# One-hot operands of the gate-matrix products: the token in front of the key, written per token

## The chip, the cores and the metric

The kernel runs on 1 core of one Trainium2 chip. The metric is device time in microseconds (us) of one execution, as the median of several runs. Engines are named as in the profile: PE is TensorE (PEld its weight loads), DVE VectorE, ACT ScalarE, POOL GpSimd, SP the engine that issues most DMAs; a q behind the name is the engine's instruction queue.

## What is computed

A float32 network on 512 tokens of 1024 channels: first two layers of short convolution and retention (with 16 meta tokens in front), then a block with two gated linear-attention mixers, and last a retrieval layer (PEER) with 16384 experts of one neuron each, and a final norm. Only the retrieval layer touches the change. Cut to that:

```python
def peer_ffn(xn, w_q, sub_keys, u, v):
    q = (xb @ w_q).reshape(128, 8, 2, 128)                    # block of 128 tokens, 8 heads, 2 sides
    s = jnp.einsum('thpd,hpnd->thpn', q, sub_keys)            # 128 sub-keys a side
    s_top, i_top = lax.top_k(s, 16)
    cand = s_top[:, :, 0, :, None] + s_top[:, :, 1, None, :]
    cand_idx = i_top[:, :, 0, :, None] * 128 + i_top[:, :, 1, None, :]
    best, pos = lax.top_k(cand.reshape(128, 8, 256), 16)
    expert = jnp.take_along_axis(cand_idx.reshape(128, 8, 256), pos, axis=-1)
    g = jax.nn.softmax(best, axis=-1)
    act = jax.nn.gelu(jnp.einsum('td,thkd->thk', xb, u[expert]), approximate=False)
    return jnp.einsum('thk,thkd->td', g * act, v[expert])
```

So each token has 128 chosen experts (8 heads by 16), each named by a first and a second key (0 to 127 each) and carrying a weight g.

## The kernel before

The 512 tokens are four tiles of 128. For the first three (NDENSE = 3) all 128 x 128 experts are computed as dense products and then weighed by a gate matrix that is zero where an expert wasn't chosen; for the last tile the chosen experts are gathered from DRAM. An "expert" e in the code is a group of 128 experts with the same first key.

Weights stream from DRAM in pieces of 128 x 1024 (class `Weights`); each piece is one task. A list of generators, the background, is advanced between tasks and between chunks of a product (`tick`), so many steps a piece as `PACE` says for the phase, always the generator at the head of the list. That gives the order of the work in the program; a scheduler that simulates the engines puts each engine's instructions in their final order, in which each engine then runs them.

The stage in question lies between the second block and the experts' phase. Three things share it:

- `top_k(i, b, sc)` ranks the keys of tile i, on DVE with small steps on ACT. `weights(i)` ends it: it transposes first keys, second keys and weights of tile i on PE (L1412) so that the 128 chosen experts lie on the partitions and the 128 tokens along the row, and writes them as float16 into `picks[i]` (keys k1 and k2, the weight in two parts w). Then it puts `gate_matrix(i)` into the background.
- `gate_matrix(i)` builds each token's matrix of 128 second keys by 128 first keys. With the chosen experts on the partitions, a one-hot matrix of the second keys, transposed, times a one-hot matrix of the first keys that is weighed by g gives that matrix by one product for each part of the weight. `rows(t0)` (L1437) compares a table `it16` of 0 to 127 with the keys of eight tokens, `weighed(t0, oh)` (L1444) multiplies the first keys' rows by both weight parts, `product(t0, oh)` (L1451) multiplies for four tokens, two products each into one bank of PSUM, and `store(t0, ps)` (L1460) copies the bank into a staging tile on ACT and writes 16 tokens at a time to DRAM (`gate_d`, L1464, on ACT's queue). A step of the generator is four tokens; the product comes two steps after the rows and the copy one step after the product. Four float16 tiles of 128 x 1024 serve eight tokens, out of ten buffers with the tag "t". In them the token is last:

```python
def wide(x, t0):
    return x[:, None, t0:t0 + 8].to_broadcast(full)          # full = [128, 128, 8]
nc.vector.tensor_tensor(out=x, in0=it16, in1=wide(k, t0), op=OP.is_equal)
nc.tensor.matmul(ps[:, t], oh[0][:, :, t0 % 8 + t], oh[j][:, :, t0 % 8 + t], start=j == 1, stop=j == 2)
```

  so a token's one-hot row, as PE reads it, has its elements 8 apart, that is 16 bytes.
- `u_task(e, direct=True)` (L1716) computes the hidden values of the first 28 experts (AHEAD) in float32, 16 pieces on PE for each; ACT applies the gelu (L1728, `hid`). These are the tasks between which the background is advanced here, 6.5 steps a piece (PACE[6]). After them the background is emptied (`W.flush`), the PSUM banks are laid out anew (`phase(2)`), the first gates are loaded from `gate_d` (`load_gates`, L1692), the ranking of the last tile follows (`late`), and the experts' phase begins (`v_task`, L1763; `weigh`, L1736, multiplies hidden values by gates on DVE).

PSUM banks of L1451 and L1716 come from the same four. The rest of the kernel, before and after this stage, isn't touched.

Of the kernel before, what the change touches and what calls it, by code (L numbers as in the profile page):

```python
# [19 lines left out]
S = 512  # L20
# [9 lines left out]
NDENSE = 3                 # tiles of tokens whose experts are all computed; the last one's are gathered  # L30
ND = 128 * NDENSE
NHN = 3                     # operands of the later products whose places hold hidden values before
AHEAD = 22 + 2 * NHN        # experts whose hidden values are computed before the first is used
PACE = (3, 1, 2, 2, 2, 3.75, 6.5, 1.5, 1, 0.7)  # steps of the background a piece, by phase
SAFTER = 1                  # gate projections of a head before its scores
QCUT = 15                   # queries of the first half that precede the second half's output projection
TICK2, TICKU = 4, 2         # chunks of a product between steps of the background
GAT = 6                     # the expert after which the gathered experts' work starts
DIRECT = (4, 8)             # query and key projections from weights that are not split, by layer
ENDS = 106                  # the expert before which the gathered ones' work is all issued  # L40
RESID = 64                  # the expert after which h is added
# banks of PSUM that each use takes turns in, by phase
# [3 lines left out]
NG = 43                     # places of both blocks' intermediate values  # L46
SLOTS = dict(sq=("q", 4))
# the second block's steps with the half of the tokens and the group: projections (FQ, KG, V, G), scores in the
# background (S), outputs of the mixers (M), their projection (O), norm (N), retrieval (Q), ends (!) and paces (P)
PLAN = "FQ00 P3 S00 P4 FQ01 S01 !N1 KG V0 G0 FQ10 S02 V1 S10 M00 FQ11 S11 G1 S12 M01 M10 O0 P8 M11 N0 Q00 O1 Q01 N1 P5 Q1"  # L50
WSCALE = 2.0 ** 14           # of the experts' weights in float16 parts
# [3 lines left out]
# columns of the per-layer table of per-channel numbers  # L55
C_BIAS, C_GN, C_PRE, C_POST, C_CW, C_CB = 0, 80, 96, 104, 112, 136
C_N = 144
# columns of the second block's table
# [11 lines left out]
class Weights:  # L70
    """Streams pieces of 1024 columns a partition, each split into two float32r parts or (direct) as it is.

    Tasks run in the order in which they were added. Steps of the generators in the
    background follow each task with a piece, `pace` of them at a time.
    """
# [23 lines left out]
    def tick(self, share):  # L99
        """Steps of the background after this share of a piece."""  # L100
        self.ticked += share
        self.credit += self.pace * share
        self.pump(int(self.credit))
        self.credit -= int(self.credit)

    def flush(self, *names):
        """Ends the generators of these names, or all of them."""
        for x in list(self.back):
            if not names or x[0] in names:
                for _ in x[1]:  # L110
                    pass
                self.back.remove(x)

    def run(self):
# [19 lines left out]
        def split(n, m):  # L134
            """The first parts of the pieces before n, the second parts of those before m."""
# [34 lines left out]
def tile_kernel(ctx: ExitStack, tc: tile.TileContext, ins, out):  # L170
# [7 lines left out]
    def phase(i):  # L178
        """The banks of PSUM, by the uses that take turns in them."""
        banks.close()  # L180
        if i is not None:
            psum["pool"] = banks.enter_context(tc.tile_pool(name=f"psum{i}", bufs=1, space=bass.MemoryType.PSUM,
                                                            reuse_waits="tile"))
            psum["roles"] = BANKS[i]
# [16 lines left out]
    def split_act(hl, src):  # L201
        """src (float32, SBUF) into the two parts of hl."""
# [9 lines left out]
    def ln(after, out, src, **k):  # L212
        """Logarithm, from the table that has the exponential too, loaded once `after` is issued."""
# [9 lines left out]
    class Sum:  # L223
        """Of squares, each step's tile squared one step later and added two steps later."""
# [17 lines left out]
    def rstd_of(r, *accs):  # L242
        """r: 1/sqrt(mean over the 1024 channels of the squares + eps), on every partition."""
# [8 lines left out]
    def rsqrt(x):  # L252
        """1/sqrt(x) of a few positive numbers a partition, by Newton's method."""
# [12 lines left out]
    def split_steps(items):  # L266
        """A generator: (tile, parts) by a function each; the parts follow one and two steps later."""
# [41 lines left out]
    # ------------------------------------------------------------ first block  # L309
    def first_block():  # L310
# [11 lines left out]
            for l in range(2):  # L322
# [19 lines left out]
                def four(c, a, b):  # L342
                    """The sum of the squares of four chunks of h, by two engines."""
# [12 lines left out]
                def pre_norm(a, b, total=None, four=four, xn=xn, x32=x32, col=col):  # L356
                    """A generator: xn[:, a:b] from h; total: the sum of the squares, if there is one."""
# [32 lines left out]
                def proj32(w, rng, x32=x32):  # L390
                    """The same from the parts' sums, for the first half of the tokens."""
# [29 lines left out]
                def v_task(h, kp, l=l, xn=xn, xm=xm, st_h=st_h):  # L421
                    def f(w):
                        if not xm:
                            # the first tokens' operands, three times the first part and once the second
# [56 lines left out]
                def s_task(h, l=l, own=own, st_h=st_h):  # L481
                    def f():
# [3 lines left out]
                        for i in range(2):  # L486
                            q, k = st_h.pop(("qh", h, i)), st_h.pop(("kh", h, i))
                            # the first tokens' keys four times
# [18 lines left out]
                        # the first tokens' scores four times: parts 0, 1, 0, 0  # L507
# [152 lines left out]
                def halve(m, own=own, st_h=st_h):  # L660
                    """The parts of y, for the first half of the tokens."""
# [33 lines left out]
                def post_norm(a, b, col=col, st_h=st_h):  # L695
                    """A generator: h[:, a:b]; returns the sum of its squares."""
# [16 lines left out]
            def norm_between(l, half):  # L713
                """From the output projection of layer l to the input of the next."""
# [8 lines left out]
            for l in range(2):  # L723
# [24 lines left out]
                # the order of the pieces in "ws" is the order of these calls  # L748
# [69 lines left out]
    # ----------------------------------------------------------- second block  # L818
# [10 lines left out]
    it16 = hp.tile([128, 128, 8], F16, name="it16")  # L829
# [7 lines left out]
    def second_block():  # L837
# [3 lines left out]
            def tables():  # L841
# [3 lines left out]
                nc.vector.tensor_copy(it16, it128[:, :, None].to_broadcast([128, 128, 8]))  # L845
# [8 lines left out]
                # the lower bound of the forget gate: softmax over the two rows of logits, its first row  # L854
# [15 lines left out]
            def pair(x):  # L870
                """Two channel chunks of one half of the tokens."""
                return x.rearrange("p (c t) -> p c t", c=2)

            def proj(w, outs, K=KD):
                """outs: (PSUM, operands): one [128, n] each chunk of channels, or its two float32r parts."""
# [14 lines left out]
            def half(s):  # L890
# [4 lines left out]
                def normed(col0, r):  # L895
                    """A generator: the operands of the projections, in parts."""
# [27 lines left out]
                def pair_task(which, c):  # L924
                    """Forget gates and queries of the first mixer, for this half."""
# [25 lines left out]
                def where(h):  # L951
                    """The pair of chunks, the chunk in it and the partitions of a head."""
# [4 lines left out]
                def scores(g):  # L957
                    """A generator: the decayed scores of the heads of a pair of chunks."""
# [8 lines left out]
                    def decay(L):  # L967
                        """To the middle of each block of 2 L tokens."""
# [11 lines left out]
                    def weigh(e, L):  # L980
                        """By the queries of the right half-blocks and the keys of the left ones."""
# [6 lines left out]
                    def right(x, L):  # L988
                        """The tokens of the right half-blocks."""
                        return x.rearrange("p (n a l) -> p n a l", a=2, l=L)[:, :, 1]  # L990

                    def products(a, b, L=None):
                        """Of each pair of tokens in a tile, or of those with a query in a right half-block."""
# [32 lines left out]
                    def whole():  # L1026
                        """To the ends of the chunks."""
# [30 lines left out]
                    # from tile 0 to tile 1, in place: keys to the end of the tile, queries to its start  # L1058
# [23 lines left out]
                    # from the first half to the second  # L1082
# [12 lines left out]
                def across(h):  # L1095
                    """Scores of the second half's queries with the first half's keys."""
# [9 lines left out]
                def outs(grp):  # L1106
                    """Of four heads, each normed, the two tiles of tokens."""
# [73 lines left out]
                def keys(c):  # L1181
                    """Scores of the sub-keys of one head and side, for both tiles of tokens."""
# [34 lines left out]
            # ---- both halves  # L1217
            def pair_both(which, c):
                """Keys and queries of the second mixer."""
# [12 lines left out]
            def low_gate():  # L1232
                """The second mixer's decay."""
# [70 lines left out]
            # Of the 16 x 16 sums of the best scores only those (a, b) with (a + 1)(b + 1) <= 16 can be  # L1304
            # among the 16 best; these rows and columns hold them, in the order of the whole table.
# [5 lines left out]
            def best16(items):  # L1311
                """A generator: (values, places, scores) each; the scores are used up."""
# [14 lines left out]
            def top_k(i, b, sc):  # L1327
                """A generator: the 16 best experts of two heads for the tokens of tile i."""
# [23 lines left out]
                # the places in the whole table  # L1352
# [15 lines left out]
                # the keys at those places: of each head and side, the one whose rank it is  # L1368
# [23 lines left out]
            def weights(i):  # L1392
                """The softmax of the best scores, and what the experts' phase needs of tile i."""
# [15 lines left out]
                if i in picks:  # L1409
# [3 lines left out]
                    # the weights, scaled, in two parts of 11 bits  # L1413
# [7 lines left out]
            def gate_matrix(i):  # L1421
                """A generator: each token's (second key, first key) matrix of weights, to DRAM."""
                k1, k2, *w = (picks[i][:, j] for j in range(4))
                full = [128, 128, 8]
                stage = []

                def wide(x, t0):
                    return x[:, None, t0:t0 + 8].to_broadcast(full)
# [530 lines left out]
```

## Time and profile before

| | us |
|---|---|
| median of 3 runs | 3429.62 (3426.72 to 3430.41) |
| span of the profiled execution | 3427.1 |
| TensorE busy in it | 3399.2 (99%) |
| VectorE busy | 2038.2 (59%) |
| ScalarE busy | 1316.0 (38%) |

The span runs from the first to the last instruction of the profiled execution; all times in the rows below are counted from its start. An operation's duration in a row reaches into the start of the next on the same engine, so start-to-start times are shorter than durations. "idle before" is time in which the engine did nothing ahead of an operation, and the name behind the arrow is what ended that. [...]

### The profile page before, as it was taken

The numbers are of one execution on the slowest core, as the hardware profiler recorded it, in microseconds if no ns is written. First come the engines' busy times: TensorE is split into PE (matmuls) and PEld (weight loads), VectorE is DVE, ScalarE is ACT, GpSimd is POOL, SyncE is SP. The second block draws the span as 40 slices with busy tenths as digits, with TensorE's granted clock in tenths as the row PEclk, the third lists the DMA queues.
The fourth block names the chain that finished last, engine by engine and source line by source line (L and its number), as shares of the span: only waits on it lengthen the run. The fifth ranks groups of instructions, "written<-read, shape, count | busy, mean of one in ns | idle before, by whom it ended". The sixth has DMA issues, their size and how long they took to land.

```text
span 3427.1 us, 51098 instructions
## 1 busy us (share of the span) xinstructions
PE 3399.2 (99%) x21063; PEld 3049.9 (89%) x21063; DVE 2038.2 (59%) x4019; ACT 1316.0 (38%) x2388; POOL 186.1 (5%) x132
## 2 busy tenths in 40 slices
PE   8999999999999999999999999999999999999999
PEld 7999999999999999999999887666679999999998
DVE  6545554335645554434656599544688888888443
ACT  5433332324533333333655433433433333333333
POOL 0000000000000000000000000000023222222000
PEclk9999999999999999999999999777899999999999
DMA  5222222223422222222321243223599898899442
GB/s 207 84 84 84 87 74 87 87 99 118 160 75 83 90 75 99 87 99 102 133 87 62 75 147 123 111 111 123 202 343 366 337 352 330 337 343 350 158 148 92
DMA packets 129962, 532.04 MB, mean 155 GB/s; under 512 B 9137, under 2 KB 60993, under 8 KB 73281
## 3 DMA queue, kind: packets, MB, share of 16 engines
q1 hardware_dynamic: 103520, 368.19, 30.2%
q0 software_dynamic: 18432, 134.23, 10.1%
q10 hardware_dynamic: 7776, 26.37, 2.0%
q8 instruction: 165, 2.70, 0.3%
q14 instruction: 69, 0.56, 0.0%
HBM read 501.48 MB, written 27.26 MB: 154 GB/s over the span
## 4 chain that ended last, share of the span: by engine, by line
PE 97%; DMA 1%; DVE 1%; ACT 1%; issue 0%; SPq 0%; DVEq 0%
PE ps L386 35%; PE ps L1763 15%; PE ps L1719 12%; PE ps L1451 5%; PE ps L454 5%; PE ps L1716 4%; PE ps L887 4%; PE ps L883 4%; PE ps L549 2%; PE ps L688 2%; PE ps L1004 2%; PE ps L1275 1%; PE ps L396 1%; PE ps L498 1%; PE ps L450 1%; DMA gates<-gate_d 1%
## 5 line engine op out<-in xcount | busy, mean ns | idle before, releaser
L143 ACT ACTIVATE hi<-raw 128x1024 fp32r<-128x1024 f32 x532 | 563.2, 1059 | 1395.6 <-PE ps L386 626.4
L151 DVE TENSOR_TENSOR lo<-raw,hi 128x1024 fp32r<-128x1024 f32 x532 | 650.1, 1223 | 752.7 <-ACT hi L143 750.8
L386 PE MATMUL ps<-xnh,hi 128*128 128x256 f32 (+1 forms) x2464 | 513.9, 283 | 0.0
L386 PE MATMUL ps<-xnl,hi 128*128 128x256 f32 (+1 forms) x2464 | 513.6, 283 | 0.0
L386 PE MATMUL ps<-xnh,lo 128*128 128x256 f32 (+1 forms) x2464 | 513.0, 283 | 0.0
L1763 PE MATMUL ps<-hi,hw 128*128 128x512 f32 x1536 | 426.0, 393 | 2.1 <-DVE hw L204 1.3
L1719 PE MATMUL ps<-hn,hi 128*128 128x384 f32 x1600 | 407.7, 336 | 0.0
L386 PEld LDWEIGHTS ps<-xnh,lo 128*128 128x128 f32 x2464 | 385.9, 189 | 0.0
L386 PEld LDWEIGHTS ps<-xnh,hi 128*128 128x128 f32 x2464 | 384.8, 188 | 1.1
L386 PEld LDWEIGHTS ps<-xnl,hi 128*128 128x128 f32 x2464 | 384.6, 188 | 0.1
L1633 POOL DMA_INDIRECT uv<-uv,idx x128 | 185.9, 1452 | 2979.5 <-PE ps L1648 2473.7
L1763 PEld LDWEIGHTS ps<-hi,hw 128*128 128x128 f32 x1536 | 286.9, 188 | 63.0 <-DVE hw L204 3.4
L1719 PEld LDWEIGHTS ps<-hn,hi 128*128 128x128 f32 x1600 | 290.0, 188 | 4.3
L1719 PE MATMUL ps<-hn,lo 128*128 128x384 f32 x800 | 268.5, 336 | 0.0
L1763 PE MATMUL ps<-lo,hw 128*128 128x512 f32 x768 | 239.2, 391 | 0.0
L1451 PE MATMUL ps<-oh 128*128 128x128 f16 x768 | 181.7, 413 | 0.0
L1716 PE MATMUL ps<-hn,raw 128*128 128x384 f32 x448 | 174.9, 554 | 0.0
L1451 PEld LDWEIGHTS <-oh 128*128 128x128 f16 x768 | 111.6, 145 | 69.0 <-issue 2.8
L1763 PEld LDWEIGHTS ps<-lo,hw 128*128 128x128 f32 x768 | 144.3, 188 | 31.3
L1661 DVE SCALAR_TENSOR_TENSOR acc<-uv,dots,acc 128x1024 f32<-128x1024 f32 x127 | 163.0, 1283 | 3.2
L1669 DVE SCALAR_TENSOR_TENSOR uv<-uv,hnT 128x1024 f32<-128x1024 f32 x128 | 155.8, 1218 | 13.0 <-DMA uv<-uv,idx 13.0
L1716 PEld LDWEIGHTS ps<-hn,raw 128*128 128x128 f32 x448 | 98.2, 223 | 69.6 <-issue 25.9
(353 smaller groups left out, 5306.8 us busy)
## 6 DMA issues: line engine op xcount, KB each, us to landing
raw<-ws SPq DMA_DIRECT2D x313, 1024.0 KB, 4.8
gate_d<-stage ACTq DMA_DIRECT2D x48, 512.0 KB, 3.2
gates<-gate_d SPq DMA_DIRECT2D x16, 1536.0 KB, 12.9
dm<-decay_m SPq DMA_DIRECT2D x8, 264.0 KB, 5.8
vb<-vbias SPq DMA_DIRECT2D x8, 256.0 KB, 5.5
dc<-decay SPq DMA_DIRECT2D x8, 256.0 KB, 5.6
uv<-uv,idx POOLq DMA_INDIRECT x128, 8.5
h<-ht SPq DMA_DIRECT2D x2, 544.0 KB, 5.3
```

Source lines behind the costliest of these rows:

```text
L143: nc.scalar.activation(hi, raw[i], AF.Copy)
L151: nc.vector.tensor_tensor(out=lo, in0=r, in1=parts[i][0].bitcast(F32), op=OP.subtract)
L386: nc.tensor.matmul(t[:, :b - a], w[wi][:, off + k, :], x[k].t[xi][:, a:b], start=(k == 0 and n == 0), stop=(k == K - 1 and n == 2))
L454: nc.tensor.matmul(p, xn[k].t[xi][:, m0:m0 + mn], w[wi][:, kk, :], start=(k == 0 and n == 0), stop=(k == KD - 1 and n == 2))
L883: nc.tensor.matmul(p, parts[0][:, k, :], x[k], start=k == 0, stop=k == K - 1)
L1451: nc.tensor.matmul(ps[:, t], oh[0][:, :, t0 % 8 + t], oh[j][:, :, t0 % 8 + t], start=j == 1, stop=j == 2)
L1633: nc.gpsimd.indirect_dma_start(out=t, out_offset=None, in_=ins["uv"], in_offset=bass.IndirectOffsetOnAxis(ap=idx[i][:, j:j + 1], axis=0))
L1661: nc.vector.scalar_tensor_tensor(out=acc, in0=v, scalar=dots[:, j:j + 1], in1=acc, op0=OP.mult, op1=OP.add)
L1669: nc.vector.scalar_tensor_tensor(out=u, in0=u, scalar=1.0, in1=hnT, op0=OP.mult, op1=OP.mult, accum_out=dots[:, j:j + 1])
L1716: nc.tensor.matmul(ps, w[0][:, k, :], tl["hn32"][k][:, :ND], start=k == 0, stop=k == KD - 1)
L1719: nc.tensor.matmul(ps, w[wi][:, k, :], tl["hn"][k][:, xi], start=(k == 0 and n == 0), stop=(k == KD - 1 and n == 2))
L1763: mm = nc.tensor.matmul(tl["acc"][t][b], h[:, hi, t * 128:(t + 1) * 128], w[vi][:, b * 512:(b + 1) * 512], start=(e == 0 and n == 0), stop ...
```

## The change

The one-hot tiles become [128, 8, 128]: the token in front, the 128 keys next to each other. The table `it16` shrinks from [128, 128, 8] to [128, 128]. `rows` only allocates, now three tiles for eight tokens (second keys; first keys weighed by the first part; by the second part). `fill` writes them token by token for the four tokens of a step: one `tensor_scalar` compares the table with the token's second key, a value for each partition, and one for each part of the weight compares it with the first key and multiplies by that part, in one operation with two values for each partition. The unweighed rows of the first keys are no longer stored. Products, copies and stores are the same in number, size and order of tokens.

```diff
-    it16 = hp.tile([128, 128, 8], F16, name="it16")
+    it16 = hp.tile([128, 128], F16, name="it16")
...
-                nc.vector.tensor_copy(it16, it128[:, :, None].to_broadcast([128, 128, 8]))
+                nc.vector.tensor_copy(it16, it128)
...
                 def rows(t0):
-                    oh = [row() for _ in range(2)]
-                    for x, k in zip(oh, (k1, k2)):
-                        nc.vector.tensor_tensor(out=x, in0=it16, in1=wide(k, t0), op=OP.is_equal)
+                    oh = [sm.tile([128, 8, 128], F16, tag="t", bufs=NT, name="oh") for _ in range(3)]
                     return oh

-                def weighed(t0, oh):
-                    parts = [row() for _ in w]
-                    for x, y in zip(parts, w):
-                        nc.vector.tensor_tensor(out=x, in0=oh[0], in1=wide(y, t0), op=OP.mult)
-                    return [oh[1], *parts]
+                def fill(t0, oh):
+                    for t in range(t0, t0 + 4):
+                        nc.vector.tensor_scalar(out=oh[0][:, t % 8], in0=it16, scalar1=k2[:, t:t + 1],
+                                                scalar2=None, op0=OP.is_equal)
+                        for x, y in zip(oh[1:], w):
+                            nc.vector.tensor_scalar(out=x[:, t % 8], in0=it16, scalar1=k1[:, t:t + 1],
+                                                    scalar2=y[:, t:t + 1], op0=OP.is_equal, op1=OP.mult)
...
-                            nc.tensor.matmul(ps[:, t], oh[0][:, :, t0 % 8 + t], oh[j][:, :, t0 % 8 + t],
+                            nc.tensor.matmul(ps[:, t], oh[0][:, t0 % 8 + t], oh[j][:, t0 % 8 + t],
                                              start=j == 1, stop=j == 2)
...
-                    if t0 % 8 == 0 and t0 < 128:
-                        raw[t0] = rows(t0)
-                    if t0 - 4 in raw:
-                        oh[t0 - 4] = weighed(t0 - 4, raw.pop(t0 - 4))
+                    if t0 < 128:
+                        if t0 % 8 == 0:
+                            oh[t0] = rows(t0)
+                        fill(t0, oh[t0 // 8 * 8])
```

## Rows read from the trace of the kernel before

**Rows 1.** The page: busy time by engine; granted clock in 40 slices.

```profile
PE 3399.2 (99%) x21063; PEld 3049.9 (89%) x21063; DVE 2038.2 (59%) x4019; ACT 1316.0 (38%) x2388; POOL 186.1 (5%) x132
...
PEclk9999999999999999999999999777899999999999
```

**Rows 2.** Stretches by window: length, busy time of each engine, granted clock, DMA.

```profile
core 0: us, PE busy (x) PEld busy (x) DVE busy (x) ACT busy (x) POOL busy (x), PEclk, DMA share, GB/s
...
2150.00:2441.00 291.00, 291.00 (x1043) 175.78 (x1042) 133.42 (x318) 115.05 (x226) 0.00 (x0) 0.72 0.30 116
2116.00:2156.00 40.00, 40.00 (x135) 23.95 (x134) 39.82 (x238) 11.36 (x30) 0.00 (x0) 1.00 0.25 90
2156.00:2432.00 276.00, 276.00 (x982) 166.43 (x981) 123.66 (x251) 107.11 (x207) 0.00 (x0) 0.72 0.31 118
```

**Rows 3.** Groups of instructions, 2150 to 2441: count, busy us, mean ns, idle before.

```profile
L1451 PE MATMUL ps<-oh 128*128 128x128 f16 x767 | 181.4, 413 | 0.0
L1716 PE MATMUL ps<-hn,raw 128*128 128x384 f32 x273 | 115.4, 587 | 0.0
L1451 PEld LDWEIGHTS <-oh 128*128 128x128 f16 x767 | 111.5, 145 | 68.9 <-issue 2.8
```

**Rows 4.** PE in order of time inside the stage: start, us, count.

```profile
2300.09 12.98 PE L1451 MATMUL ps<-oh 128*128 128x128 f16 x55
2312.89 7.05 PE L1716 MATMUL ps<-hn,raw 128*128 128x384 f32 x16
```

**Rows 5.** PE in order of time, before and behind the one-hot products.

```profile
2126.78 23.39 PE L1716 MATMUL ps<-hn,raw 128*128 128x384 f32 x72
...
2441.28 23.19 PE L1716 MATMUL ps<-hn,raw 128*128 128x384 f32 x64
...
2473.55 1.04 PE L1648 MATMUL ps<-ident,hn 128*128 128x128 f32 x8
...
2477.18 1.99 PE L1763 MATMUL ps<-hi,hw 128*128 128x512 f32 x8
```

**Rows 6.** Waits of DVE, 2116 to 2432: us in total, times, longest.

```profile
DVE oh L1437 <- PE ps L1451: 118.5, 28, 7.8
DVE oh L1444 <- PE ps L1451: 29.1, 15, 4.7
DVE picks L1417 <- ACT picks L1416: 3.3, 1, 3.3
```

**Rows 7.** Groups of DVE operations by shape, the whole span: busy us, mean ns.

```profile
L1437 DVE TENSOR_TENSOR oh<-it,picks 128x1024 f16<-128x1024 f16 x96 | 63.1, 687 | 118.9 <-PE ps L1451 118.5
...
L986 DVE TENSOR_TENSOR e<-e,k 128x256 f32<-128x256 f32 x36 | 15.1, 418 | 0.0
...
L941 DVE TENSOR_SCALAR f<-f,omlb,lb 128x256 f32<-128x256 f32 x8 | 2.9, 410 | 10.5 <-ACT f L938 10.5
...
L1363 DVE TENSOR_SCALAR mf<-pf 128x32 f32<-128x32 f32 x16 | 2.8, 174 | 0.0
...
L1645 DVE SCALAR_TENSOR_TENSOR hn<-h,cols,rstd 128x128 f32<-128x128 f32 x8 | 2.2, 341 | 0.0
...
L944 DVE TENSOR_SCALAR k<-f 128x512 f32<-128x512 f32 x4 | 1.7, 427 | 0.1
...
L1408 DVE TENSOR_TENSOR gwt<-gwt,sm 128x128 f32<-128x128 f32 x3 | 0.8, 282 | 0.0
...
L1659 DVE TENSOR_SCALAR acc<-uv,dots 128x1024 f32<-128x1024 f32 x1 | 0.7, 745 | 0.0
```

**Rows 8.** DVE in order of time inside the stage: two in a row.

```profile
2311.62 1.29 DVE L1437 TENSOR_TENSOR oh<-it,picks 128x1024 f16<-128x1024 f16 x2
```

**Rows 9.** Two of the stretches, DVE operations on the one-hot tiles alone.

```profile
2116.00:2156.00 40.00, 8.27 (x13) 1.00 0.25 90
2156.00:2432.00 276.00, 113.05 (x179) 0.72 0.31 118
```

**Rows 10.** ACT in order of time: the last copy of the stage.

```profile
2442.84 0.61 ACT L1460 ACTIVATE stage<-ps 128x256 f32<-128x256 f32 x1
```

**Rows 11.** Instructions on the gates: duration min/median/max, first and last start.

```profile
L1736 DVE TENSOR_TENSOR hid<-hid,gates x128: 546/551/559, 2453.7 to 3406.1; 128x384 f32<-128x384 f32 x128
```

More of the change, by code (lines that the diff above doesn't have):

```diff
@@ L1423, in gate_matrix @@
                 k1, k2, *w = (picks[i][:, j] for j in range(4))
-                full = [128, 128, 8]
                 stage = []
-                def wide(x, t0):
-                    return x[:, None, t0:t0 + 8].to_broadcast(full)
-                def row():
-                    return sm.tile([128, 128, 8], F16, tag="t", bufs=NT, name="oh")
                 def rows(t0):
-                    oh = [row() for _ in range(2)]
-                    for x, k in zip(oh, (k1, k2)):
-                        nc.vector.tensor_tensor(out=x, in0=it16, in1=wide(k, t0), op=OP.is_equal)
-                    return oh
-                def weighed(t0, oh):
-                    parts = [row() for _ in w]
-                    for x, y in zip(parts, w):
-                        nc.vector.tensor_tensor(out=x, in0=oh[0], in1=wide(y, t0), op=OP.mult)
-                    return [oh[1], *parts]
+                    oh = [sm.tile([128, 8, 128], F16, tag="t", bufs=NT, name="oh") for _ in range(3)]
+                    return oh
+                def fill(t0, oh):
[5 more added lines that the diff above has]
+                                                    scalar2=y[:, t:t + 1], op0=OP.is_equal, op1=OP.mult)
                 def product(t0, oh):
@@ L1464, in store @@
                             nc.scalar.dma_start(gate_d[:, (128 * i + t0) // 16, j * 1024:(j + 1) * 1024], stage[j])
-                raw, oh, ps = {}, {}, {}
+                oh, ps = {}, {}
                 for t0 in range(0, 128 + 12, 4):
```

## Prediction

> **What bounds the kernel now.** I read the page first: TensorE is busy for 99% of the span, and the granted clock is below its upper level in one place alone, the slices just past two thirds [rows 1]. So the question is what TensorE does there. The stretches by window give that place edges: from 2150 to 2441 us the mean granted clock is 0.72, TensorE never pauses and VectorE is busy 133 of 291 us [rows 2]. The groups of instructions of that stretch show two things only: 767 of the 768 one-hot products (L1451) and 273 pieces of the early experts' products (L1716) [rows 3]. In order of time the products come in runs such as 55 in 12.98 us, which is 12.98 less one duration of 0.41, over 54 gaps: 0.233 us from start to start. Each has a weight load of its own, of 0.145 us [rows 3]. All products together take 768 x 0.233 = 179 us, over half the stretch. [...] VectorE meanwhile waits for TensorE: 118.5 + 29.1 us, for tiles that the products have not yet freed [rows 6]. So the stage goes at TensorE's pace, and that pace is a strided one: both operands of L1451 step by 16 bytes from element to element.
>
> **The change, part by part.** *The products* stay 768 in number, same columns, same type. No row shows a contiguous float16 product of this size. The nearest are float32 products of 128 columns (L1648): eight in 1.04 us, each 0.27 long, so 0.11 apart [rows 5]. From above, 0.233 stays if the stride isn't the cause. From below, products of 512 columns run 0.229 apart (eight in 1.99 us, 0.39 long) [rows 5], so 128 columns need 0.057. I take 0.11, the row of the same columns: 84 us for 179, a gain of 95 us on TensorE (0 to 135). [...]
>
> *VectorE's part* is where this is decided. Removed: 192 operations of 128x1024 (96 on L1437, 96 like them on L1444), 0.687 us each, two back to back in 1.29, so 0.605 from start to start, an overlap of 0.08 [rows 7, 8]: 116 us. Added: 3 operations of 128x128 for each of 384 tokens, 1152 in all. Each has three prices.
> A fixed one: tensor_scalar with immediates takes 0.427 us for 512 float32 (L944) and 0.174 for 32 (L1363) [rows 7]; the slope is 0.53 ns an element, and 0.174 - 0.08 - 0.017 leaves 0.077 us.
> The elements: float32 tensor_tensor costs 1.06 ns an element (0.418 for 256, 0.282 for 128), float16 tensor_tensor about 0.52 (0.605 less the fixed part over 1024), float32 tensor_scalar 0.53 [rows 7]. Two bytes halve it and tensor_scalar halves it; I take both at once, 0.26 ns, 0.034 us for 128. No row has the combination, so it is bounded: 0.53 if only one halving holds (0.068), and 1.06 (0.135) if neither does [rows 7].
> The scalars: a scalar that is read per partition isn't free. With one, 128x128 takes 0.341 (L1645) where an operation without takes 0.282 (L1408); with one, 1024 take 0.745 (L1659), 0.045 more than 0.08 + 0.077 + 1024 x 0.53 ns; with two, 256 take 0.410 (L941) where 0.08 + 0.077 + 0.136 = 0.293 is left without, so 0.117 for two [rows 7]. I take 0.06 each; from below it is nothing, should float16 scalars or this operation not pay it.
> An operation with the key alone then costs 0.077 + 0.06 + 0.034 = 0.171, one with key and weight 0.231; a token 0.171 + 2 x 0.231 = 0.633, and 384 tokens **243 us** where there were 116. With one halving it is 282, with none 360, without the price of the scalars 128.
>
> *The sum.* VectorE begins on the operands at about 2116 us. Until 2156 it is full: 39.8 us busy, 8.3 of them on the operands, so 31.6 for other work (ranking for the tiles of tokens that follow). From 2156 to 2432 it is busy 123.7, of them 113.1 on the operands, leaving 10.6, plus a wait of 3.3 for ScalarE [rows 2, 6, 9]. So 46 us of VectorE's time stays, in the same in-order queue. If VectorE never waits for TensorE, the last operand is written at 2116 + 46 + 243 = 2405. Behind it come eight products (0.9) and two copies, which ScalarE makes at some 0.6 each: about 2408. Now the last copy starts at 2442.84 and lasts 0.6 [rows 10]: 2443.5. That is **36 us** earlier.
> Does TensorE keep up? From 2113 it has, up to the end of the operands, 448 - 64 = 384 pieces of L1716 (the other 64 come after the last one-hot product [rows 5]), 384 x 0.323 = 124, plus 84, plus at most the 27 of the lower clock: 2113 + 235 = 2348. It does, with nearly 60 us in hand; its waits then stand on VectorE's operands, and what it now loses to the lower clock lies in that slack and is not counted as a gain. ScalarE, busy 115 us in the stretch [rows 2], fits too. Behind the stage nothing is regained: the 64 pieces of L1716 (23.2 us) cover the way of the gates through DRAM, which are first used at 2453.7 [rows 5, 11]; both shift with the stage.
> Smaller edits: the table it16 shrinks from 1024 to 128 columns, one cast, below 1 us, and it lies long before. Three tiles in place of four for eight tokens out of ten buffers let VectorE be some three groups ahead in place of two and a half, so that TensorE's L1716 runs of 5 to 7 us don't stop it; were that cover gone, each of some 17 runs would cost up to 2 us. No transfer moves; the stores to gate_d stay on ScalarE's queue behind its copies. Where TensorE waits for an operand, the next expert's L1716 stands behind it in order; ScalarE's hid copies alone wait for that, and nothing else needs them in this stage.
> Span 3427.1 - 36 = 3391. The median of the runs lies 2.5 us above the profiled span (3429.6); with the same distance, **3394 us**.
>
> **The rivals.**
> *TensorE stays the bound.* If scalars cost nothing, VectorE needs 116 + 12 = 128 us, ends at 2290, and the stage ends when TensorE does: 2113 + 124 + 84 + some 20 for the lower clock = 2341, so about 100 us earlier, 3327 us. For it: float16 scalars aren't in the trace. Against it: three different rows show the price. [...]
> *VectorE is at break-even.* With only one halving, 282 us: the last copy ends at 2116 + 46 + 282 + 3 = 2447, 4 us later than now, 3433 us. For it: no tensor_scalar on float16 is in the trace. Against: the two halvings are seen apart and on different operations.
> *VectorE becomes a worse bound than TensorE was (slower).* At 1.06 ns an element the operands take 360 us: 2525, some 82 us later, 3511 us. The point from which this decides is a mean of 0.242 us an operation: (2443.5 - 3 - 2116 - 46) / 1152. My mean is 0.211, which is near. A little added to each operation, such as a wait in front, reaches it: 0.04 more is already 10 us on the wrong side. Against it: float32 tensor_scalar from SBUF takes 0.53 ns with a scalar as well (L1659).
> *The change doesn't do what it says.* If 0.233 comes from something other than the stride, TensorE's stage stays as it is, VectorE's 243 us hide behind it, and the time is 3430.
>
> **How the numbers follow.** A difference of 0.2% (7 us) is about what a measurement of this kernel can tell. Chances: VectorE as the bound at 0.21 us an operation, 3394 us (3380 to 3410), 0.54; TensorE still the bound, 3327, 0.13; a price between those two, 3345 to 3380, 0.05; break-even, 3433, 0.11; unchanged pace of the products, 3430, 0.06; slower for VectorE's sake by more than 0.2%, 3440 to 3511, 0.11. Faster: the first three, 0.72, less a little for break-even's spread: 0.71. Same: 0.14. Slower: 0.15. A range from 3335 to 3436 takes in all but the slow cases and most of the fastest: about 8 in 10.
>
> **What would show it.** In the profile after, the operations on the one-hot operands should last 0.25 and 0.31 us each (start to start plus 0.08), 1152 of them; VectorE should be full from 2116 to about 2405 with no waits for the products; TensorE should show idle time in front of L1451, ended by VectorE. The products should come 0.11 us apart within a run. L1716 may still have runs at the lower clock. If VectorE still waits for TensorE, the scalars' price was wrong; if operations last 0.35 and more, the elements' price was; if products stay at 0.233, the stride was.

## The result and the profile after

| | before | after |
|---|---|---|
| median, us | 3430.0 | 3378.9 |
| ratio, 95% interval | | 0.985 (0.9838 to 0.9862) |
| span of the profiled execution, us | 3427.1 | 3377.2 |
| VectorE busy in it, us | 2038.2 | 2152.3 |

51 us faster, where 36 were forecast. The page of the kernel after, busy time by engine, granted clock in 40 slices and the chain that ended last, against [rows 1]:

```profile
PE 3313.5 (98%) x21063; PEld 2989.4 (89%) x21063; DVE 2152.3 (64%) x4979; ACT 1302.9 (39%) x2388; POOL 184.7 (5%) x132
...
PEclk9999999999999999999999999988999999999999
...
PE 84%; DVE 12%; DMA 2%; ACT 1%; issue 1%; POOL 0%; DVEq 0%; ACTq 0%; POOLq 0%
PE ps L386 36%; PE ps L1755 13%; PE ps L1711 12%; PE ps L454 5%; DVE oh L1436 5%; PE ps L887 3%; DVE oh L1433 2%; PE ps L549 2%; PE ps L688 2%; PE ps L1004 2%; PE ps L1275 1%; PE ps L396 1%; PE ps L498 1%; PE ps L883 1%; PE ps L450 1%; DMA uv<-uv,idx 1%
```

In the page of the kernel before, the chain by engine was:

```profile
PE 97%; DMA 1%; DVE 1%; ACT 1%; issue 0%; SPq 0%; DVEq 0%
```

VectorE, which hardly showed in the chain of a TensorE-bound kernel, now holds 12% of it, over half of that in the two lines that write the operands (L1436 and L1433). The instructions on the one-hot tiles (duration in ns min/median/max, first and last start), where [rows 3, 7] had the old ones:

```profile
L1436 DVE TENSOR_SCALAR oh<-it,picks x768: 258/315/325, 2115.5 to 2380.8; 128x128 f16<-128x128 f16 x192
L1443 PEld LDWEIGHTS <-oh x768: 95/98/119, 2147.2 to 2386.4; 128*128 128x128 f16 x192
L1443 PE MATMUL ps<-oh x768: 216/219/290, 2147.5 to 2386.5; 128*128 128x128 f16 x192
L1433 DVE TENSOR_SCALAR oh<-it,picks x384: 235/255/265, 2114.8 to 2380.4; 128x128 f16<-128x128 f16 x192
its engine sat idle before it (us, times) until:
  DVE oh L1436: 40.5, 134
  DVE oh L1433: 26.2, 95
```

The two sums of idle time add up the waits of the products (15.1 us) and of their weight loads (51.7). The same view of the staging tile, for the copies out of PSUM:

```profile
L1452 ACT ACTIVATE stage<-ps x192: 580/630/663, 2152.6 to 2388.3; 128x256 f32<-128x256 f32 x192
```

The wait has turned round: no longer does VectorE wait for products [rows 6], the products wait for VectorE. Its last operand comes at 2381 in place of 2432 us, the last copy starts at 2388.3 in place of 2442.84 [rows 10]. Two stretches of the kernel after by window (columns as in [rows 2]), all engines:

```profile
2116.00:2156.00 40.00, 38.87 (x151) 23.51 (x150) 39.47 (x243) 9.81 (x22) 0.00 (x0) 1.00 0.24 83
2156.00:2382.00 226.00, 198.34 (x996) 111.27 (x996) 226.00 (x1109) 100.57 (x215) 0.00 (x0) 0.83 0.41 151
```

The same two windows, VectorE's instructions on the one-hot tiles alone:

```profile
2116.00:2156.00 40.00, 15.49 (x75) 1.00 0.24 83
2156.00:2382.00 226.00, 218.57 (x1072) 0.83 0.41 151
```

VectorE is busy in all of the 226 us, and 218.6 of them go into the operands. TensorE idles for 28, about half of it in waits for VectorE. In order of time, VectorE within the stage of the kernel after (start, duration, count last):

```profile
2272.80 0.26 DVE L1433 TENSOR_SCALAR oh<-it,picks 128x128 f16<-128x128 f16 x1
2272.96 0.55 DVE L1436 TENSOR_SCALAR oh<-it,picks 128x128 f16<-128x128 f16 x2
2273.41 0.26 DVE L1433 TENSOR_SCALAR oh<-it,picks 128x128 f16<-128x128 f16 x1
```

And TensorE there, a run of products that found its operands ready:

```profile
2154.52 1.06 PE L1443 MATMUL ps<-oh 128*128 128x128 f16 x16
```

From one token to the next it is 0.61 us: 0.16 for the operation with the key, 0.225 each for the two with key and weight (over the stage 0.163 and 0.223). The products of the run are (1.06 - 0.22) / 15 = 0.056 us apart, where they were 0.233.

### The profile page after: what moved, and what is told of

Its sections match the earlier page's. It is cut to its first block, busy times and chain, and to the rows that moved or that the text cites. A ratio compares the mean times of both kernels' runs of the same rounds, so it can differ in the third digit from the quotient of the medians.

```text
span 3377.2 us, 52075 instructions
## 1 busy us (share of the span) xinstructions
PE 3313.5 (98%) x21063; PEld 2989.4 (89%) x21063; DVE 2152.3 (64%) x4979; ACT 1302.9 (39%) x2388; POOL 184.7 (5%) x132
## 4 chain that ended last, share of the span: by engine, by line
PE 84%; DVE 12%; DMA 2%; ACT 1%; issue 1%; POOL 0%; DVEq 0%; ACTq 0%; POOLq 0%
PE ps L386 36%; PE ps L1755 13%; PE ps L1711 12%; PE ps L454 5%; DVE oh L1436 5%; PE ps L887 3%; DVE oh L1433 2%; PE ps L549 2%; PE ps L688 2%; PE ps L1004 2%; PE ps L1275 1%; PE ps L396 1%; PE ps L498 1%; PE ps L883 1%; PE ps L450 1%; DMA uv<-uv,idx 1%
## 5 line engine op out<-in xcount | busy, mean ns | idle before, releaser
L1755 PE MATMUL ps<-hi,hw 128*128 128x512 f32 x1536 | 428.9, 395 | 10.3 <-DVE hw L204 9.3
L1755 PEld LDWEIGHTS ps<-hi,hw 128*128 128x128 f32 x1536 | 288.2, 189 | 72.8 <-DVE hw L204 12.0
L1755 PE MATMUL ps<-lo,hw 128*128 128x512 f32 x768 | 239.9, 392 | 0.0
L1436 DVE TENSOR_SCALAR oh<-it,picks 128x128 f16<-128x128 f16 x768 | 204.9, 313 | 0.0
L1708 PE MATMUL ps<-hn,raw 128*128 128x384 f32 x448 | 172.0, 545 | 1.8 <-ACT stage L1452 1.0
L1755 PEld LDWEIGHTS ps<-lo,hw 128*128 128x128 f32 x768 | 144.9, 189 | 32.0
L1708 PEld LDWEIGHTS ps<-hn,raw 128*128 128x128 f32 x448 | 94.1, 215 | 67.1 <-issue 20.9
L1711 PEld LDWEIGHTS ps<-hn,lo 128*128 128x128 f32 x800 | 150.0, 188 | 0.1
```

Of the source, the lines that this page charges most:

```text
L1436: nc.vector.tensor_scalar(out=x[:, t % 8], in0=it16, scalar1=k1[:, t:t + 1], scalar2=y[:, t:t + 1], op0=OP.is_equal, op1=OP.mult)
L1708: nc.tensor.matmul(ps, w[0][:, k, :], tl["hn32"][k][:, :ND], start=k == 0, stop=k == KD - 1)
L1711: nc.tensor.matmul(ps, w[wi][:, k, :], tl["hn"][k][:, xi], start=(k == 0 and n == 0), stop=(k == KD - 1 and n == 2))
L1755: mm = nc.tensor.matmul(tl["acc"][t][b], h[:, hi, t * 128:(t + 1) * 128], w[vi][:, b * 512:(b + 1) * 512], start=(e == 0 and n == 0), stop ...
```

## The experiments

The theory is the prediction's: the 16-byte steps set TensorE's pace before, and the price of VectorE's operations, scalars above all, sets the stage's pace now. The change has two parts, the layout and the writing per token, so each was also made alone. e1_strided, e3_immediates, e4_one_part, e6_wide_contiguous and e7_rank_first were run once each, so a difference of some 7 us (0.2%) between two of them says nothing by itself.

**The writing alone (e1_strided).** Tiles with the token last, written per token.

```diff
-oh = [sm.tile([128, 8, 128], F16, tag="t", bufs=NT, name="oh") for _ in range(3)]
+oh = [sm.tile([128, 128, 8], F16, tag="t", bufs=NT, name="oh") for _ in range(3)]
...
-out=oh[0][:, t % 8], ... out=x[:, t % 8]
+out=oh[0][:, :, t % 8], ... out=x[:, :, t % 8]
...
-nc.tensor.matmul(ps[:, t], oh[0][:, t0 % 8 + t], oh[j][:, t0 % 8 + t],
+nc.tensor.matmul(ps[:, t], oh[0][:, :, t0 % 8 + t], oh[j][:, :, t0 % 8 + t],
```

> The changed kernel with the token last again in the one-hot tiles (16 bytes from element to element), still written per token by tensor_scalar. Theory (the stride of the operands set TensorE's pace before): the products are back at about 0.233 us from start to start, and VectorE's operations, which now write with steps, cost one halving less, 0.196 and 0.256 us in place of 0.163 and 0.223, 272 us in all; both engines then need about what TensorE needed before, and the time is 3425 to 3445 us. Rival (the pace of before came from the wide operations that made eight tokens' operands at once, so that products came in bursts): the products stay near 0.056 us and the time lies at 3379 plus what VectorE's operations lose, at most 3415 us.

Measured: 3479.4 us, slower than both kernels. Products and operations on the one-hot tiles in order of time:

```profile
2299.67 11.55 PE L1443 MATMUL ps<-oh 128*128 128x128 f16 x49
...
2300.14 0.71 DVE L1433 TENSOR_SCALAR oh<-it,picks 128x128 f16<-128x128 f16 x1
2300.43 1.01 DVE L1436 TENSOR_SCALAR oh<-it,picks 128x128 f16<-128x128 f16 x2
2301.03 0.71 DVE L1433 TENSOR_SCALAR oh<-it,picks 128x128 f16<-128x128 f16 x1
```

49 products in 11.55 us are 0.232 apart: the stride is back and so is the pace, and the rival (bursts) falls. Nor does the pace come from the lower clock, which such runs meet. Two runs of the kernel before, each with its window:

```profile
2150.01 3.87 PE L1451 MATMUL ps<-oh 128*128 128x128 f16 x16
2150.00:2154.00 4.00, 4.00 (x18) 2.58 (x17) 4.00 (x34) 0.96 (x4) 0.00 (x0) 1.00 0.00 2
2165.64 4.61 PE L1451 MATMUL ps<-oh 128*128 128x128 f16 x19
2166.00:2170.00 4.00, 4.00 (x19) 2.49 (x18) 1.89 (x3) 2.15 (x4) 0.00 (x0) 0.50 0.57 221
```

They are (3.87 - 0.41) / 15 = 0.231 us apart at the upper level (granted clock 1.00, a share of full speed) and (4.61 - 0.41) / 18 = 0.233 at the lower (0.50). But the expectation for VectorE was wrong: 0.89 us a token, 0.29 for each operation, the one with one scalar and the two with two alike. Neither 0.196 nor 0.256 fits: written in 16-byte steps, an operation takes longer than either, and a second scalar adds nothing to it. 1152 x 0.29 is over 330 us, and VectorE bounds this kernel too, which is why it is 48 us slower than before (3431.0 on the same chip) and not equal. So the prediction's slower rival came about here by another cause, the stepped writes: 0.29 lies beyond its point of decision of 0.242 us, by 0.048 x 1152 = 55 us.

**The layout alone (e6_wide_contiguous).** The four wide operations of before, writing contiguous rows.

```diff
-full = [128, 128, 8]
+full = [128, 8, 128]
...
-return x[:, None, t0:t0 + 8].to_broadcast(full)
+return x[:, t0:t0 + 8, None].to_broadcast(full)
...
-nc.vector.tensor_tensor(out=x, in0=it16, in1=wide(k, t0), op=OP.is_equal)
+nc.vector.tensor_tensor(out=x, in0=it16[:, None].to_broadcast(full), in1=wide(k, t0), op=OP.is_equal)
```

The table shrinks and the products read rows as in the changed kernel.

> The contiguous layout of the changed kernel, written by the wide tensor_tensor operations of the kernel before (eight tokens at once; the token's key or weight is repeated along the innermost dimension). [...] Rival (the operations keep 0.60 us): TensorE bounds and the time is about 3295 us, and neither the per-token form nor the pairs were needed.

Measured: 3372.1 us. VectorE in order of time:

```profile
2253.17 2.34 DVE L1437 TENSOR_TENSOR oh<-it,picks 128x1024 f16<-128x1024 f16 x2
```

Two in 2.34 us with a duration of 1.21: 1.13 from start to start, 218 us in all, so the rival (0.60 kept) falls. A value repeated along the innermost dimension nearly doubles the operation, from 0.605 [rows 8] to 1.13 (e2_pairs, below, repeats the table too, but along an outer dimension, and keeps 0.60). Less the prediction's fixed 0.077 us that is 1.03 ns an element, an estimate from this run and [rows 7], about what float32 took there (1.06) and twice what float16 did (0.52). The wide form then costs VectorE a little less than the per-token form of the change (234 us). The time hardly shows that: the last operand comes at 2376 us, 5 earlier than in the changed kernel though the operands cost 16 us less (218 for 234), and the last copy ends at 2388.0 where it ended at 2388.9. Of the 7 us, 6 come behind the stage, and one run can't tell such a difference. Of the two parts only the layout pays; the writing per token is a way to get it, and no cheaper than the wide form.

**The scalars' price (e3_immediates).** Constants in place of the scalars:

```diff
-scalar1=k2[:, t:t + 1], ... scalar1=k1[:, t:t + 1], scalar2=y[:, t:t + 1],
+scalar1=5.0, ... scalar1=7.0, scalar2=0.5,
```

> The changed kernel with constants in place of the scalars read per partition, so the gate matrix holds nothing of the keys and weights: that part of the computation is left out, the number and size of operations stay. Theory (a scalar read per partition costs 0.06 us each): all 1152 operations last about 0.105 us from start to start, 121 us in all; TensorE becomes the bound and the time is about 3305 us. Rival (the 0.163 and 0.223 us are a fixed price of the operation or of its second step): the operations keep them and the time stays at 3379 us.

Measured: 3297.0 us. VectorE in order of time:

```profile
2250.68 0.32 DVE L1436 TENSOR_SCALAR oh<-it 128x128 f16<-128x128 f16 x2
2250.89 0.22 DVE L1433 TENSOR_SCALAR oh<-it 128x128 f16<-128x128 f16 x1
2250.99 0.32 DVE L1436 TENSOR_SCALAR oh<-it 128x128 f16<-128x128 f16 x2
2251.19 0.22 DVE L1433 TENSOR_SCALAR oh<-it 128x128 f16<-128x128 f16 x1
```

Three operations in 0.305 us, 0.102 each with or without a second step. With one scalar it was 0.163, with two 0.223: 0.06 for each, on float16 as on the float32 rows that the prediction took it from. 0.12 more for two thirds of 1152 operations and 0.06 for the rest are 115 us of VectorE, and 82 us of the time hang on them. Then TensorE binds: VectorE waits 21 us for its products again.

**Is VectorE really the bound (e4_one_part)?** The third operation for each token is left out.

```diff
-for x, y in zip(oh[1:], w):
+for x, y in zip(oh[1:], w[:1]):
...
-nc.tensor.matmul(ps[:, t], oh[0][:, t0 % 8 + t], oh[j][:, t0 % 8 + t],
+nc.tensor.matmul(ps[:, t], oh[0][:, t0 % 8 + t], oh[1][:, t0 % 8 + t],
```

> The changed kernel without the operation for the weight's second part (384 of 1152); the second product reads the first part's tile again, so the number of products is the same and the low part of the weights is left out. Theory (VectorE bounds the stage): its work falls from 234 to 148 us, the stage ends some 70 to 85 us earlier until TensorE binds, and the time is 3300 to 3315 us. Rival (TensorE or ScalarE's copies bound the stage behind VectorE's busy look): less than 20 us of it arrives, 3360 us or more.

Measured: 3300.4 us. 86 us of VectorE's work less, 79 us of the time. In this kernel's view of the one-hot tiles:

```profile
L1433 DVE TENSOR_SCALAR oh<-it,picks x384: 215/276/363, 2116.9 to 2302.8; 128x128 f16<-128x128 f16 x192
```

The last operand moved from 2381 to 2303 us; the 192 copies and 768 products were the same. The rival falls.

**A layout that both engines like (e2_pairs, e5_quads).** By the runs so far VectorE is fast with tokens innermost, so that key and weight step by one (0.60 us an operation for 1.13), and TensorE with a token's elements close together (0.056 us a product for 0.233). Two tokens behind each key give both (e5_quads has four):

```diff
-it16 = hp.tile([128, 128, 8], F16, name="it16")
+it16 = hp.tile([128, 128, 2], F16, name="it16")
...
-full = [128, 128, 8]
+full = [128, 4, 128, 2]
...
-return x[:, None, t0:t0 + 8].to_broadcast(full)
+return x[:, t0:t0 + 8].rearrange("p (g t) -> p g t", t=2)[:, :, None, :].to_broadcast(full)
...
-nc.vector.tensor_tensor(out=x, in0=it16, in1=wide(k, t0), op=OP.is_equal)
+nc.vector.tensor_tensor(out=x, in0=it16[:, None].to_broadcast(full), in1=wide(k, t0), op=OP.is_equal)
...
-nc.tensor.matmul(ps[:, t], oh[0][:, :, t0 % 8 + t], oh[j][:, :, t0 % 8 + t],
+q, r = divmod(t0 % 8 + t, 2)
+nc.tensor.matmul(ps[:, t], oh[0][:, q, :, r], oh[j][:, q, :, r],
```

> The kernel before, with the two innermost dimensions of the one-hot tiles cut to two tokens behind each key (4 bytes from key to key for a token), still written by the four wide tensor_tensor operations for eight tokens. Theory (TensorE was slowed by reads 16 bytes apart, and VectorE only pays for being called per token): products at 0.056 to 0.07 us, VectorE's operations at 0.60 us as before, 116 us in all; TensorE bounds the stage with 145 (L1716) + 43 + about 20 for the lower clock from 2113 on, so the experts' phase begins near 2321 in place of 2401 us, and the time is 3300 to 3315 us, faster than both kernels. Rival 1 (only contiguous rows are read at full pace): products at 0.233 and 3430 us. [...]

Measured: 3295.4 us, 0.9606 of before (0.959 to 0.9622), so 84 us faster than the changed kernel too. It is also some 5 us faster than the expected range, which had 20 us for the lower clock that weren't paid (below).

> As the kernel with pairs of tokens behind each key, but with four (8 bytes from key to key for a token, so two of its elements in 16 bytes). Theory (what counts is that more than one element comes from the same 16 bytes): products at about 0.058 us, VectorE's operations at 0.60 us, and 3290 to 3300 us as with pairs. Rival (the pace falls steadily with the stride): products near 0.12 us, so some 46 us more on TensorE, which bounds this stage, and about 3340 us.

Measured: 3320.2 us, 0.9679 of before (0.9663 to 0.9695); the rival holds for the pace. Of its 46 us against the pairs 25 arrive; TensorE, which waited 13 us in the stage with pairs, mostly for ScalarE's copies, waits for nothing here. Products of the kernel with pairs in order of time:

```profile
2216.26 2.46 PE L1453 MATMUL ps<-oh 128*128 128x128 f16 x40
```

Those of the kernel with quads:

```profile
2224.52 5.83 PE L1453 MATMUL ps<-oh 128*128 128x128 f16 x48
```

VectorE's operations on the one-hot tiles of the kernel with pairs, in order of time:

```profile
2219.15 1.29 DVE L1437 TENSOR_TENSOR oh<-it,picks 128x1024 f16<-128x1024 f16 x2
```

(2.46 - 0.22) / 39 = 0.057 us with steps of 4 bytes; (5.83 - 0.30) / 47 = 0.118 with 8; VectorE keeps its 0.60. With the other kernels that is a series for one product with its weight load: steps of 2 bytes 0.056, 4 bytes 0.057, 8 bytes 0.118, 16 bytes 0.233. With steps of 8 bytes two elements lie in the same 16, and the pace is half of that at 4 bytes, so the theory of e5_quads falls: from 4 to 16 bytes the time goes with the step (the runs with 2, 4 and 8 bytes at the upper level of the clock, those with 16 at either). Of the kernel with pairs, the stage by window:

```profile
2150.00:2304.00 154.00, 141.32 (x1047) 97.87 (x1046) 129.61 (x313) 99.33 (x224) 0.00 (x0) 1.00 0.56 214
```

The clock stays at its upper level, the 154 us were 291 [rows 2], and TensorE is the busiest engine again.

**The work that left the stage (e7_rank_first).** VectorE's work other than the operands took 32 us between the first and the last of them, not 46. Sums over VectorE's ranking lines (1300 to 1412) say where it went: before, 42 us of ranking fell between the first and last operand and 13 behind; after, 29 and 25. What moved is the last tile's ranking. Here it goes in front:

```diff
-if 2 * s + t < NDENSE:
-    W.later(top_k(2 * s + t, b, x), name="top")
-else:
-    experts.late.append(top_k(2 * s + t, b, x))
+W.later(top_k(2 * s + t, b, x), name="top")
```

> The changed kernel with the ranking of the last tile, 25 us of which VectorE does behind the last one-hot operand, moved in front of the one-hot operands together with the other tiles' ranking; nothing is left out. Theory (where VectorE bounds the stage, every microsecond of its other work inside counts in full, and ranking that slipped behind it is the gain that the sum missed): the last operand comes about 25 us later, near 2406 us, and the time is 3396 to 3406 us. Rival (VectorE's ranking is hidden wherever it stands, and the sum was off elsewhere): within 5 us of 3379 us.

Measured: 3395.9 us, 17 more than the changed kernel, at the edge of what was expected. In its view of the one-hot tiles (its line numbers are 3 lower, so this is the operation with two scalars):

```profile
L1433 DVE TENSOR_SCALAR oh<-it,picks x768: 296/297/427, 2160.3 to 2409.3; 128x128 f16<-128x128 f16 x192
```

And of the staging tile:

```profile
L1449 ACT ACTIVATE stage<-ps x192: 579/629/651, 2185.3 to 2410.3; 128x256 f32<-128x256 f32 x192
```

The last operand comes 28 us later, the last copy 22, the end 17. So in a stage that VectorE bounds the place of its other work counts for most of its length, and the rival (hidden wherever it stands) falls.

## Why the prediction was right, and what was off

*The bound now.* Right, though no row of before shows it: 0.233 us a product was the stride (e1_strided brings it back, e2_pairs takes it away without any of the per-token writing).

*The products.* I took 0.11 from a float32 row; they run at 0.056, the lower end of the range. It should have changed nothing here: with 0.11, TensorE's sum still ends at 2348 us, before VectorE's last operand at 2381. No run shows that.

*VectorE's price.* Right where the runs can tell its terms apart, a little high in sum: 0.163 and 0.223 where I had 0.171 and 0.231, 234 us where I had 243. Immediates show 0.102 for fixed part and elements together (forecast 0.111) and 0.06 a scalar (forecast 0.06). That both halvings hold at once, which no row had shown, is what 0.102 speaks for: at 0.53 ns an element the 128 alone would take 0.068 and leave 0.034 for the fixed part, where I had read 0.077; no run measures the two apart. The rival in which TensorE stays the bound would have come true without the scalars, faster even than its 3327 us (e3_immediates, 3297).

*The sum.* The right mechanism with one term mis-sized. The forecast was that the last copy ends at 2408, it ends at 2388.9. By terms: the operands 9 us less; VectorE's other work 32 in place of 46, so 14 less, the largest error; the first operand 1 us sooner; behind the last operand 8 us in place of 3, since a run of the early experts' products stands between the last one-hot products, 5 more. The time, 3379 us, lies just outside the band of its own branch (3380 to 3410), though the branch is the one that came.

The 14 were the step "46 us of VectorE's time stays": I read off what ran within the stage before and took it as bound to stay. In the changed kernel 13 us of ranking went behind the stage instead, where TensorE has 44 pieces of L1708 to cover it:

```profile
2386.53 14.41 PE L1708 MATMUL ps<-hn,raw 128*128 128x384 f32 x44
```

That VectorE is full doesn't by itself push ranking out. In e6_wide_contiguous it is just as full; by window, all engines and VectorE's instructions on the one-hot tiles alone:

```profile
2156.00:2376.00 220.00, 161.07 (x1005) 105.80 (x1004) 220.00 (x302) 98.40 (x225) 0.00 (x0) 0.86 0.40 153
2156.00:2376.00 220.00, 204.73 (x179) 0.86 0.40 153
```

Yet by the same sums 42 us of ranking stay between its first and last operand and 13 behind, as before the change, and there the step holds: 2116 + 42 + 218 = 2376, where its last operand ends. Which work stands where is fixed by the scheduler's simulation before the kernel runs, so the likely cause is what that takes the new operations to cost; no run varies it by itself, and this stays open. e7_rank_first shows what the place is worth.

*Behind the stage.* "Nothing is regained" held, and a little was lost. The last copy ends 54.5 us earlier, the span 49.9. The experts' phase starts 64 us earlier, at 2401.2 in place of 2465.0 [rows 5], since only 44 of those pieces are left, and then waits for gates and for VectorE: in waits of TensorE behind the stage, "PE ps L1755 <- DVE hw L204" has 9.3 us where it had 1.3. The gates come no sooner behind the last copy: the first three loads of them are issued 2.2, 15.0 and 27.9 us after it, where it was 1.4, 14.2 and 26.5 before. From the last copy to the end it is 988.3 us after and 983.7 before. Of that, TensorE has 9 us less work with L1708 (38 pieces left for 61), but idles 8 us more (16.4 for 8.7), and the experts' products take 4 us more, at a granted clock of 0.91 to 0.97 in stretches of 20 us from 2400 to 2460, where the same phase had 1.00 before; that is most of the 4.6 us. The ranking that now follows the stage is not shown to cause it: e1_strided, with as much ranking behind, has 984.4, and e3_immediates, with as little as before, 989.7. Why TensorE waits more stays open.

*The clock.* In the kernel before, by windows of 1 us, the granted clock is 1.00 from 2300 to 2306 us, 0.50 from 2307 to 2316 and 1.00 from 2317 to 2320: it falls within the run of 55 products, and the 16 pieces of L1716 behind it begin at the lower level [rows 4]. The 27 us that the sum has for it are 115.4 us for 273 pieces [rows 3] less the 88 that they take at 0.323 us each, the pace of the 72 pieces of [rows 5], 2126 to 2150, where the clock is 1.00. As forecast, L1708 still meets the lower level (mean granted clock 0.83 in the stage), and that lies in slack: VectorE waits 0.5 us in all of it. In e2_pairs (2150 to 2304) and e5_quads (2113 to 2350) the clock is 1.00 throughout the stage and the loss of 27 us is gone. Waits of TensorE don't tell the cases apart: before, it never paused and the mean was 0.72 [rows 2]; in e2_pairs it idled 13 of 154 us at 1.00. In these rows the level fell in runs of products 0.233 us apart, and where products came in twos every 0.61 us (the changed kernel has 1.00 from 2248 to 2250 us, 0.85 from 2250 to 2252 and 0.50 from 2252 to 2254), and stayed up with runs 0.057 to 0.118 apart (1.00 in e2_pairs and e5_quads).

*The rivals.* Break-even stood at 0.242 us an operation, 279 us in all. The changed kernel needs 234 and gains; e1_strided needs over 330 and is slower than before; e4_one_part (148) and e3_immediates (118) gain more. All come out as that point says.

## What to carry to other kernels

Before an operand's layout is changed for one engine, price the other engine's instructions by their count: 1152 small operations with one or two scalars cost together twice what the 192 wide ones before them did (234 us for 116), and took back over 80 of the 135 us that the layout is worth here. Look for a layout between: two elements side by side were enough for VectorE to keep 0.60 us an operation, and 4-byte steps cost TensorE nothing (0.057 us a product for 0.056). And when the bound moves to an engine that had idle time, don't take its other work as bound to stay where it was: 13 us of it left the stage here and none in e6_wide_contiguous, with VectorE equally full.

## What the runs showed of the hardware that I had not expected

- A product of 128 columns in float16 with its own weight load runs at 0.056 us when both operands are contiguous; steps of 4, 8 and 16 bytes give 0.057, 0.118 and 0.233, the last at a granted clock of 1.00 and of 0.50 alike.
- tensor_scalar on 128 float16 costs 0.102 us with immediates and 0.06 us more for each scalar read per partition; written with 16-byte steps it costs 0.29 with one scalar or two.
- A float16 tensor_tensor of 1024 keeps 0.60 us with only two elements in the innermost dimension, and takes 1.13 when one operand is repeated along it.
